# An output piece that no longer ends its stage: a hybrid trunk layer on one core, with two tiles and one flag moved

## The chip, the cores and the metric

The kernel runs on one NeuronCore of a Trainium2 chip. The time is that of one execution on the device, in microseconds; the figure of a kernel is the median of its runs. A profile is one more execution with the hardware profiler on; its span is the time from the first to the last instruction.

## What is computed

One layer of a streaming encoder over 2048 rows of 1024 channels, in float32. Cut to what matters here:

```
h = rmsnorm(x) * (1 + scale) + shift
p = h @ w_in                                  # one projection, cut among the branches
A = latent attention (8 heads, block-causal)  # softmax over all earlier rows
B = gMLP gating inside 128-row blocks
C = RWKV-7 recurrence over the rows           # chunked: 64-row chunks, state carried on
proj = each branch * silu(z) @ w_br           # three projections
merged = sum(proj * sigmoid(gate))
y = merged @ w_out
out = x + gate * rmsnorm(y)
```

## The kernel before

The 2048 rows are cut into four super-blocks of 512 (`s` = 0 to 3). For each `s` there are two stages, one after the other: `wkv(s)`, the recurrence of the super-block, and `attention(s)`. In the text they are recurrence 0 to 3 and attention 0 to 3. Each stage opens a pool of SBUF tiles (`pl`) and closes it at its end, so the tiles of the next stage can take the same memory.

All matrix products of 512 columns are made as three fp32r products of split operands (`mm3`: high by high, high by low, low by high). In the trace they are rows such as `pd<-hh,wh`, and the text calls them dense matmuls. The split weights are kept in DRAM (`kept`) and loaded again, 256 KB for the high and 256 KB for the low part of four k-tiles, that is for 12 dense matmuls (`again`, `wgran`). The ring that they are loaded into has nine places for high and low parts together; by the turns of its three tags the high part of a weight pair waits for the pair five before it to be used up, and the low part for the pair four before it.

TensorE's order is not written by hand. While the program is built, a planner (`Pace`) keeps generators ("threads") of ranks -1 to 4, estimates when each one's operands are ready, and lets one after the other issue its next step (`run`). The recurrence and the attention have low ranks; the projections that fill the gaps stand in two queues, `todo` (rank 3, what the next super-block needs first) and `later` (rank 4). The order that comes out is fixed: on the chip each engine works through its own list in that order and waits where an operand is late. SyncE issues nearly all DMAs, in its order too; a DMA that waits for a semaphore holds up every DMA behind it.

The last steps of a super-block, its three output pieces (`finish_units`), run as filler in the next recurrence: those of super-block `s - 1` in `wkv(s)`, for `s` = 1, 2 and 3. The last of them is `rows()`: it makes eight pieces of 128 x 512, for each of which it loads `y` and `x`, makes `y * rs + x` on VectorE, and stores to `out`. Its tiles come from the ring `f` of the stage's pool, three buffers for all its users. When all eight have been issued it sets `old[s, 3]`, and `wkv` ends only then:

```
pace.run(lambda: done[0] == 4 and (s == 0 or (s - 1, 3) in old), ...)   # line 1317, in wkv(s)
```

`done[0] == 4` says that the recurrence's four head pairs are issued. The recurrence's last steps on TensorE are the transpositions `pss<-consts,Y`; VectorE makes their result ready and SyncE stores it (`yr_d<-y`). Then `attention(s)` starts with the loads of its first head (`stg<-q_d`, `stg<-k_d`, `stg<-kp_d`, `vf<-v_d`), which ScalarE and GpSimd split into high and low parts (`qh`, `kh`; `ql`, `kl`), and its first matmuls are `pss<-kh,qh` and `pss<-kl,qh`. `x` and `y` of `rows()`, the weights and these loads all stand in SyncE's one list. Nearly every instruction is shown with line 120, that of the helper that records it.

Of the kernel before, what the change touches and what calls it, by code (L numbers as in the profile page):

```python
# [11 lines left out]
F32 = mybir.dt.float32  # L12
# [9 lines left out]
P = 128  # L22
# [284 lines left out]
def trunk(ctx, tc, io, out):  # L307
# [5 lines left out]
    def pool(name, bufs=1, space=None, stack=ctx):  # L313
        kw = {} if space is None else {"space": space}
        return pace.pool(stack.enter_context(tc.tile_pool(name=name, bufs=bufs, reuse_waits="tile", **kw)), bufs)
# [6 lines left out]
    sm = pool("sm", 2)  # L322
# [17 lines left out]
    def pt():  # L340
        return pace.ring("t", ps_t.tile([P, 512], F32, tag="t", name="pst"))
# [18 lines left out]
    def rstd_of(dst, src, mul, eps, n):  # L360

        tmp = sm.tile([P, 16], F32, tag="rst", name="rst", bufs=4)
        G.tensor_scalar(tmp[:, :n], src, mul, eps, op0=ALU.mult, op1=ALU.add)
        G.tensor_tensor(out=dst, in0=tmp[:, :n], in1=nhalf.broadcast_to([P, n]), op=ALU.pow)
# [215 lines left out]
    def gemm(w, c0, rhs, nk=KD, r0=0):  # L580

        yield (RD, *rhs[0])
        pace.lock = pace.cur
        o = pd()
        for kg in range(nk // 4):
            pace.early = EAR
            src = w[r0 + kg * 512:r0 + (kg + 1) * 512, c0:c0 + P].rearrange("(k p) c -> p k c", p=P)
            h, l = wgran((w.tensor.name, w.offset, r0 + kg * 512, c0), lambda raw: SY.dma_start(raw, src))
            pace.early = 0.0
            pace.forget(h, l)  # L590
            for k in range(4):
                kk = kg * 4 + k
                rh, rl = rhs[kk]
                yield (rh, rl)
                mm3(o, h[:, k, :], l[:, k, :], rh, rl, kk == 0, kk == nk - 1)
        pace.lock = None
        return o
# [96 lines left out]
    old = {}  # L694
# [866 lines left out]
    def operand(src, b):  # L1561

        yield ()
        for g in range(4):
            y = sm.tile([P, 512], F32, tag="z2", name="yg", bufs=3)
            SY.dma_start(y, src[g])
            b.append(br_split(y))
# [10 lines left out]
    def finish_units(s, pl):  # L1578

        bm, b0, b1 = [], [], []  # L1580
        ss = pl.tile([P, 4, 8], F32, name="ss")
        cnt = [0]

        def ft(name):
            return pl.tile([P, 512], F32, tag="f", name=name, bufs=FB)

        def merge(d):
            t = sm.tile([P, 512], F32, tag="gt", name="gt", bufs=2)
            SY.dma_start(t, gd[s % 2][0][d])
            q = ft("p12")  # L1590
            SY.dma_start(q, pp[s % 2][1][d])
            op = yield from gemm(w_br[0], d * P, bm, nk=4)
            V.scalar_tensor_tensor(t, t, 1.0, op, op0=ALU.add, op1=ALU.mult)
            ME.tensor_tensor(out=t, in0=t, in1=q, op=ALU.add)
            SY.dma_start(mg_d[s][d], t)

        def out0(e):
            o = yield from gemm(w_out, e * P, b0, nk=4)
            f = ft("yo")
            A.activation(f, o, AF.Copy)  # L1600
            SY.dma_start(yo_d[s][e], f)

        def out1(e):
            f = ft("yo")
            SY.dma_start(f, yo_d[s][e])
            gp = pl.tile([P, 1, P], F32, tag="gp", name="gp", bufs=2)
            SY.dma_start(gp[:, 0, :], gpg_d[:, e * P:(e + 1) * P])
            o = yield from gemm(w_out, e * P, b1, nk=4, r0=512)
            V.tensor_tensor(out=f, in0=o, in1=f, op=ALU.add)
            pace.spawn(1, back(e, f, gp))  # L1610

        def back(e, f, gp):
            yield (RT, f)
            o = pt()
            for j in range(4):
                PE.transpose(out=o[:, j * P:(j + 1) * P], in_=f[:, j * P:(j + 1) * P], identity=ident)
            jk = pl.tile([P, P], BF16, tag="jf", name="jf")
            for j in range(4):
                A.activation(jk, o[:, j * P:(j + 1) * P], AF.Square, accum_out=ss[:, j, e:e + 1])
            w = ft("yw")  # L1620
            V.tensor_tensor(out=w.rearrange("p (j c) -> p j c", j=4), in0=o.rearrange("p (j c) -> p j c", j=4),
                            in1=gp.broadcast_to([P, 4, P]), op=ALU.mult)
            SY.dma_start(y_d[s][:, e * P:(e + 1) * P].rearrange("(j p) c -> p j c", p=P), w.rearrange("p (j c) -> p j c", j=4))
            cnt[0] += 1
            if cnt[0] == 8:
                pace.spawn(0, rows())

        def rows():
            rs = sm.tile([P, 4], F32, tag="ors", name="ors")
            V.tensor_reduce(out=rs, in_=ss, axis=AX.X, op=ALU.add)  # L1630
            rstd_of(rs, rs, 1.0 / D, EPS, 4)
            for j in range(4):
                for i in range(2):
                    rows_, cs = slice(j * P, (j + 1) * P), slice(i * 512, (i + 1) * 512)
                    y, x = ft("y"), ft("x")
                    SY.dma_start(y, y_d[s][rows_, cs])
                    SY.dma_start(x, io["x"][0, s * SB + j * P:s * SB + (j + 1) * P, cs])
                    V.scalar_tensor_tensor(y, y, rs[:, j:j + 1], x, op0=ALU.mult, op1=ALU.add)
                    SY.dma_start(out[0, s * SB + j * P:s * SB + (j + 1) * P, cs], y)
                    yield (y,)  # L1640
            old[s, 3] = True

        return [[lambda: operand(ym_d[s], bm)] + [lambda d=d: merge(d) for d in range(8)],
                [lambda: operand(mg_d[s][0:4], b0)] + [lambda e=e: out0(e) for e in range(8)],
                [lambda: operand(mg_d[s][4:8], b1)] + [lambda e=e: out1(e) for e in range(8)]]
# [111 lines left out]
```

## Time and profile before

| | |
|---|---|
| median of 3 runs | 3095.43 us (3093.91 to 3096.95) |
| profiled execution, its own time | 3098.93 us |
| its span | 3096.6 us |
| granted TensorE clock, mean | 0.97 |
| TensorE busy (matmuls) | 2877.7 us, 93% of the span |
| VectorE busy | 1714.8 us, 55% |
| DMA queue of SyncE, share of 16 engines | 66.0% |

The profiled execution is 3.5 us longer than the median and 2.3 us longer than its span. "Busy" is time with an instruction in work; the idle time of an engine is listed before the instruction that ended it, with what that instruction waited for. The granted clock is a share of 2.4 GHz; a stretch at 1.2 GHz counts as half.

### The profile page before, as it was taken

The page shows a single profiled execution, that of the slowest core. Times are in us where ns is not written, and L with a number is a line of the kernel's source. Part 1 is how long each engine was busy: PE and PEld are TensorE (multiplying, and loading weights), DVE is VectorE, ACT ScalarE, POOL GpSimd, SP SyncE. Part 2 cuts the span into 40 slices and gives each one's busy share as a digit, 9 for nine tenths or more (in the row PEclk, how much of TensorE's full clock was granted, in tenths as well). Part 3 has the DMA queues.
Part 4 walks back from the last instruction along what each step waited for, and adds up shares of the span by engine and source line. Part 5 has one row for each costly group of instructions (what it writes and reads, how often), then busy time and mean ns, then how long its engine had stood idle before and what let it go on. Part 6 is the DMA issues. An engine that isn't in the chain of part 4 may idle for free.

```text
span 3096.6 us, 49478 instructions
## 1 busy us (share of the span) xinstructions
PE 2877.7 (93%) x16924; PEld 2330.6 (75%) x16924; DVE 1714.8 (55%) x4574; ACT 1235.2 (40%) x2868; POOL 598.8 (19%) x606
## 2 busy tenths in 40 slices
PE   5889988989989999999999998998899999899998
PEld 4667766777867777878877777887787677788886
DVE  6426675466257753466357653446645765356653
ACT  4325433444233433444333323454433333267641
POOL 3122232332021211131011101113100110222210
PEclk8999999989999999999999999999999999999999
DMA  7888755877766689765665578655557556844456
GB/s 270 260 273 252 223 176 164 268 237 244 231 211 196 198 252 286 223 203 173 211 210 174 167 236 266 201 164 187 160 168 243 179 158 215 263 143 134 124 183 218
DMA packets 521383, 645.84 MB, mean 209 GB/s; under 512 B 142160, under 2 KB 254892, under 8 KB 521132
## 3 DMA queue, kind: packets, MB, share of 16 engines
q1 hardware_dynamic: 520960, 642.64, 66.0%
q8 instruction: 134, 2.20, 0.3%
q14 instruction: 117, 0.96, 0.1%
q10 hardware_dynamic: 172, 0.05, 0.0%
HBM read 457.69 MB, written 184.81 MB: 207 GB/s over the span
## 4 chain that ended last, share of the span: by engine, by line
PE 59%; DVE 5%; DMA 4%; ACT 2%; issue 1%; POOL 1%; SPq 1%; POOLq 0%; DVEq 0%; ACTq 0%
PE pd L120 36%; PE pss L120 10%; PE pst L120 9%; PE pso L120 4%; DMA x<-in_x 1%; SPq L120 1%; DVE X L120 1%; DVE tx L120 0%; DMA tg<-gate_d 0%; DMA wr<-in_w_out 0%; DMA wl<-kept 0%; DMA yo<-yo_d 0%; ACT Y L120 0%; DMA xtb<-xd 0%; DMA wh<-kept 0%
## 5 line engine op out<-in xcount | busy, mean ns | idle before, releaser
L120 PE MATMUL pd<-hh,wh 128*128 128x512 f32 x1952 | 810.6, 415 | 16.7 <-ACT wh L120 6.4
L120 PE MATMUL pd<-hh,wl 128*128 128x512 f32 x1952 | 775.2, 397 | 7.8 <-POOL wl L120 5.9
L120 PE MATMUL pd<-hl,wh 128*128 128x512 f32 x1952 | 773.9, 396 | 2.8 <-DVE hl L120 1.8
L120 PEld LDWEIGHTS pd<-hh,wh 128*128 128x128 f32 x1952 | 373.3, 191 | 105.5 <-issue 13.2
L120 PEld LDWEIGHTS pd<-hh,wl 128*128 128x128 f32 x1952 | 372.2, 191 | 95.6 <-POOL wl L120 9.7
L120 PEld LDWEIGHTS pd<-hl,wh 128*128 128x128 f32 x1952 | 374.5, 192 | 71.1 <-DVE hl L120 3.6
L120 DVE TENSOR_TENSOR pw<-pst,ph 128x512 fp32r<-128x512 f32 (+2 forms) x352 | 196.3, 568 | 248.9 <-ACT ph L120 247.5
L120 ACT ACTIVATE ph<-pst 128x512 fp32r<-128x512 f32 (+2 forms) x352 | 171.5, 497 | 247.6 <-PE pst L120 211.2
L120 PE MATMUL pd<-brh,wh 128*128 128x512 f32 x576 | 252.3, 438 | 18.8 <-DVE gt L120 9.0
L120 PE MATMUL pd<-brh,wl 128*128 128x512 f32 x576 | 229.8, 399 | 0.6 <-POOL wl L120 0.6
L120 PE MATMUL pd<-brl,wh 128*128 128x512 f32 x576 | 230.2, 400 | 0.0
L120 DVE TENSOR_SCALAR_CACHE_REDUCE p<-pss 128x512 f32<-128x512 f32 (+2 forms) x320 | 191.2, 607 | 69.2 <-PE pss L120 65.2
L120 ACT ACTIVATE p<-p,nm 128x512 f32<-128x512 f32 (+3 forms) x288 | 189.7, 660 | 82.8 <-DVE nm L120 82.4
L120 POOL TENSOR_TENSOR wl<-wr,wh 128x512 fp32r<-128x512 f32 x98 | 131.2, 1341 | 435.4 <-ACT wh L120 347.5
L120 ACT ACTIVATE wh<-wr 128x512 fp32r<-128x512 f32 x162 | 101.1, 628 | 230.3 <-PE pd L120 89.0
L120 PE MATMUL pst<-consts,p 128*128 128x128 f32 x1088 | 162.4, 274 | 10.7 <-DVE za L120 5.8
L120 PE MATMUL pso<-ph,v 128*128 128x256 f32 x576 | 152.8, 288 | 0.0
L120 PEld LDWEIGHTS pd<-brh,wh 128*128 128x128 f32 x576 | 111.2, 193 | 52.3 <-issue 13.8
L120 PEld LDWEIGHTS pst<-consts,p 128*128 128x128 f32 x1088 | 128.8, 141 | 27.3 <-issue 12.0
L120 PE MATMUL pso<-pw,v 128*128 128x256 f32 x576 | 146.4, 283 | 1.2 <-DVE pw L120 1.2
L120 PE MATMUL pss<-kh,qh 96*128 96x512 f32 (+2 forms) x320 | 129.3, 404 | 18.2 <-ACT kh L120 15.2
L120 POOL TENSOR_TENSOR kl<-stg,kh 96x512 fp32r<-96x512 f32 x80 | 103.4, 1296 | 220.5 <-ACT kh L120 214.2
(295 smaller groups left out, 4820.7 us busy)
## 6 DMA issues: line engine op xcount, KB each, us to landing
wh<-kept SPq DMA_DIRECT2D x486, 256.0 KB
wl<-kept SPq DMA_DIRECT2D x486, 256.0 KB
kept<-wh SPq DMA_DIRECT2D x162, 256.0 KB
kept<-wl SPq DMA_DIRECT2D x162, 256.0 KB
wr<-in_w_in SPq DMA_DIRECT2D x120, 256.0 KB
gate_d<-gt SPq DMA_DIRECT2D x64, 256.0 KB
part_d<-gt SPq DMA_DIRECT2D x64, 256.0 KB
p<-part_d SPq DMA_DIRECT2D x64, 256.0 KB
```

Source lines behind the costliest of these rows:

```text
L120: r = f(*a, **k)
```

## The change

`old[s, 3]` is set when `rows()` starts instead of when it ends, and the tiles `y` and `x` of `rows()` come from the pool `sm`, which stays open through all stages, with one buffer each, instead of from the stage's ring `f`. So `wkv(s)` may end when the recurrence is done and `rows()` has begun, and the rest of the eight pieces is issued in `attention(s)`. The computation is the same.

```diff
             rs = sm.tile([P, 4], F32, tag="ors", name="ors")
             V.tensor_reduce(out=rs, in_=ss, axis=AX.X, op=ALU.add)
             rstd_of(rs, rs, 1.0 / D, EPS, 4)
+            old[s, 3] = True
             for j in range(4):
                 for i in range(2):
                     rows_, cs = slice(j * P, (j + 1) * P), slice(i * 512, (i + 1) * 512)
-                    y, x = ft("y"), ft("x")
+                    y, x = (sm.tile([P, 512], F32, tag=n, name=n[1], bufs=1) for n in ("ry", "rx"))
                     SY.dma_start(y, y_d[s][rows_, cs])
                     SY.dma_start(x, io["x"][0, s * SB + j * P:s * SB + (j + 1) * P, cs])
                     V.scalar_tensor_tensor(y, y, rs[:, j:j + 1], x, op0=ALU.mult, op1=ALU.add)
                     SY.dma_start(out[0, s * SB + j * P:s * SB + (j + 1) * P, cs], y)
                     yield (y,)
-            old[s, 3] = True
```

What the planner makes of it: TensorE's list is the same, instruction for instruction, but for three stretches, each from the end of a recurrence (1, 2 and 3) to the end of the attention behind it. Between the last transposition of the recurrence and the first matmul of the attention there stood 243, 198 and 198 dense matmuls; now there stand 45, 36 and 30. The others stand inside the attention and behind it: runs of 96, 81 and 123 dense matmuls now end the three stretches. The number of separate runs of dense matmuls in the three stretches goes from 151, 131 and 99 to 174, 139 and 113. (24 matmuls of two weight pairs go from the second stretch to the first.)

TensorE at the passage from recurrence 2 to attention 2, before: the last dense matmuls and the first three of the attention (`wh` and `wl` are the weight pair, `kh`, `kl`, `qh`, `ql` the split key and query).

```order
L120 MATMUL pd_19646<-hh_13728,wl_19668 128x512 [waits DMAHW5_49]
L120 MATMUL pd_19646<-hh_13730,wh_19667 128x512
L120 MATMUL pd_19646<-hl_13731,wh_19667 128x512
L120 MATMUL pd_19646<-hh_13730,wl_19668 128x512
L120 MATMUL pss_19677<-kh_19569,qh_19562 128x512 [waits PE_49,Activation_49]
L120 MATMUL pss_19677<-kl_19570,qh_19562 128x512 [waits Pool_49]
L120 MATMUL pss_19677<-kh_19569,ql_19563 128x512
```

And now, at the same place:

```order
L120 MATMUL pd_19406<-hh_14191,wl_19408 128x512
L120 MATMUL pd_19406<-hh_14193,wh_19407 128x512
L120 MATMUL pd_19406<-hl_14194,wh_19407 128x512
L120 MATMUL pd_19406<-hh_14193,wl_19408 128x512
L120 MATMUL pss_19427<-kh_19313,qh_19306 128x512 [waits PE_49,Activation_49]
L120 MATMUL pss_19427<-kl_19314,qh_19306 128x512 [waits Pool_49]
L120 MATMUL pss_19427<-kh_19313,ql_19307 128x512
```

The three matmuls wait for the same things as before, but the pair ahead of them is `wh_19407`, the third pair behind the recurrence's last transposition, where it was the seventeenth.

SyncE's list at the same passage, before, from the store of the last of the eight pieces to the attention's first load:

```order
L120 DMA out<-y_19495 128x512 [waits DMAHW0_49,DVE_49]
L120 DMA wh_19804<-kept_3861 128x512 [waits DMAHW1_49,PE_49]
L120 DMA yg_21833<-yr_d2_365 128x512 [waits DMAHW2_49]
L120 DMA wl_19805<-kept_3862 128x512 [waits DMAHW3_49,PE_49]
L120 DMA stg_19560<-q_d2_325 96x512 [waits DMAHW4_49]
```

And now, from the load of the third piece's `y` to the attention's first load:

```order
L120 DMA y_19270<-y_d1_360 128x512 [waits DMAHW6_49,DMAHW3_49]
L120 DMA wl_19424<-kept_2724 128x512 [waits DMAHW4_49,PE_49]
L120 DMA x_19271<-in_x 128x512 [waits DMAHW5_49]
L120 DMA wh_19463<-kept_2892 128x512 [waits PE_49]
L120 DMA wl_19464<-kept_2893 128x512 [waits DMAHW7_49,PE_49]
L120 DMA yr_d2_365<-y_19295 128x512 [waits DMAHW0_49,DVE_49]
L120 DMA out<-y_19270 128x512 [waits DMAHW1_49,DVE_49]
L120 DMA ut_19288<-sg_d2_341 128x512 [waits DMAHW2_49,DVE_49]
L120 DMA x_19391<-in_x 128x512 [waits DMAHW5_49,DMAHW3_49]
L120 DMA stg_19304<-q_d2_325 96x512 [waits DMAHW4_49]
```

The attention's first load stood behind the store of the eighth piece; now it stands behind the store of the recurrence's last tile and of the third piece. Five of the eight pieces are behind it. In stage 1 it is behind the fourth piece's store, in stage 3 behind the load of the fourth piece's `y`.

## Rows read from the trace of the kernel before

**Rows 1.** The profile's page, its first part: busy time of each engine, its share of the span, and its number of instructions.

```profile
PE 2877.7 (93%) x16924; PEld 2330.6 (75%) x16924; DVE 1714.8 (55%) x4574; ACT 1235.2 (40%) x2868; POOL 598.8 (19%) x606
```

**Rows 2.** Busy time of each engine in four stretches (microseconds from the span's start; behind each engine's busy time its number of instructions), with the granted TensorE clock as a share of full speed, the mean busy share of the 16 DMA engines and what they moved. First the last 46 us of the recurrence stage of super-block 2, then the first 18 us of attention 2 and of attention 3, then the passage from recurrence 0 to attention 0.

```profile
core 0: us, PE busy (x) PEld busy (x) DVE busy (x) ACT busy (x) POOL busy (x), PEclk, DMA share, GB/s
1848.00:1894.00 46.00, 45.37 (x202) 37.48 (x202) 17.13 (x26) 7.13 (x12) 0.00 (x0) 1.00 0.90 302
1894.00:1912.00 18.00, 9.76 (x29) 7.16 (x29) 1.81 (x7) 6.41 (x13) 7.09 (x7) 0.72 0.70 206
2682.00:2700.00 18.00, 9.66 (x29) 7.03 (x28) 1.97 (x5) 4.75 (x10) 8.92 (x9) 0.72 0.63 159
578.00:600.00 22.00, 19.71 (x79) 16.04 (x78) 6.57 (x23) 11.66 (x28) 7.44 (x9) 0.84 1.02 322
```

**Rows 3.** TensorE in order of time at the passage from recurrence 2 to attention 2: start, duration, engine, line, operation, out<-in, partitions x elements; in brackets the idle time before the instruction and what ended it. The first row is the last transposition of the recurrence, the next two are the ends of a run of 57 dense matmuls, the last two are the first matmuls of the attention.

```profile
1848.63 0.63 PE L120 MATMUL pss<-consts,Y 128*128 128x128 f32 x4 [0.85 <-DVE Y L120]
...
1855.03 0.39 PE L120 MATMUL pd<-hh,wl 128*128 128x512 f32 x1
...
1867.73 0.39 PE L120 MATMUL pd<-hl,wh 128*128 128x512 f32 x1
...
1901.20 0.80 PE L120 MATMUL pss<-kh,qh 96*128 96x512 f32 x1 [7.02 <-ACT kh L120]
1903.21 0.80 PE L120 MATMUL pss<-kl,qh 96*128 96x512 f32 x1 [1.22 <-POOL kl L120]
```

**Rows 4.** The same view at the passage from recurrence 3 to attention 3. The last row is the last of 14 single 512-column matmuls (the first is that of 2690.25) whose duration is above 0.55 us.

```profile
2637.26 0.60 PE L120 MATMUL pss<-consts,Y 128*128 128x128 f32 x4
...
2690.25 0.79 PE L120 MATMUL pss<-kh,qh 96*128 96x512 f32 x1 [7.45 <-ACT kh L120]
2691.93 0.79 PE L120 MATMUL pss<-kl,qh 96*128 96x512 f32 x1 [0.89 <-POOL kl L120]
...
2692.94 0.63 PE L120 MATMUL pd<-hh,wh 128*128 128x512 f32 x1
2693.37 0.63 PE L120 MATMUL pd<-hl,wh 128*128 128x512 f32 x1
...
2697.21 0.56 PE L120 MATMUL pd<-brl,wh 128*128 128x512 f32 x1
```

**Rows 5.** The same view at the passage from recurrence 1 to attention 1.

```profile
1153.72 0.63 PE L120 MATMUL pss<-consts,Y 128*128 128x128 f32 x4 [0.51 <-DVE Y L120]
...
1209.28 0.40 PE L120 MATMUL pss<-kh,qh 96*128 96x512 f32 x1
...
1218.64 0.50 PE L120 MATMUL pss<-kh,qh 96*128 96x512 f32 x1 [3.00 <-DVE p L120]
```

**Rows 6.** SyncE's DMA queue in order of time (start, duration of the issue) at the passage from recurrence 2 to attention 2.

```profile
1855.21 0.34 SPq L120 DMA_DIRECT2D out<-y  x1
...
1856.07 0.48 SPq L120 DMA_DIRECT2D yr_d<-y  x1
...
1886.21 0.41 SPq L120 DMA_DIRECT2D x<-in_x  x1
...
1891.67 0.34 SPq L120 DMA_DIRECT2D out<-y  x1
...
1893.51 0.42 SPq L120 DMA_DIRECT2D stg<-q_d  x1
```

**Rows 7.** The same queue at the two other passages: the store of the recurrence's last tile in stage 1 and in stage 3.

```profile
1158.01 0.32 SPq L120 DMA_DIRECT2D yr_d<-y  x1
...
2643.77 0.46 SPq L120 DMA_DIRECT2D yr_d<-y  x1
```

**Rows 8.** ScalarE in order of time: the first split of the query tile in attention 2.

```profile
1899.96 0.63 ACT L120 ACTIVATE qh<-stg 96x512 fp32r<-96x512 f32 x1 [11.88 <-DMA stg<-q_d]
```

**Rows 9.** The passage from recurrence 0 to attention 0, TensorE and SyncE's DMA queue: the last transposition of the recurrence, the store of its last tile, the first load of the attention, and the first two matmuls of the attention.

```profile
578.48 0.60 PE L120 MATMUL pss<-consts,Y 128*128 128x128 f32 x4
...
581.41 0.32 SPq L120 DMA_DIRECT2D yr_d<-y  x1
...
584.39 0.33 SPq L120 DMA_DIRECT2D stg<-q_d  x1
...
590.06 0.33 PE L120 MATMUL pss<-kh,qh 96*128 96x128 f32 x1 [0.75 <-ACT kh L120]
591.92 0.48 PE L120 MATMUL pss<-kl,qh 96*128 96x128 f32 x1 [1.54 <-POOL kl L120]
```

**Rows 10.** What ended VectorE's and the other engines' idle time before the 46 instructions that touch the tile `ors` (the row scales of an output piece): total microseconds, times; the row of the loads of `x`.

```profile
  DMA x<-in_x: 38.7, 16
```

**Rows 11.** What SyncE's DMA queue waited for from 1840 to 1894 us: total, times, longest.

```profile
SPq L120 <- DVE y L120: 13.1, 6, 3.1
SPq L120 <- PE pd L120: 12.2, 12, 1.6
SPq L120 <- DMA out<-y: 0.8, 1, 0.8
```

**Rows 12.** What TensorE waited for inside attention 2, from 1915 to 2301 us (the longest row).

```profile
PE pd L120 <- DVE gt L120: 6.9, 4, 3.9
```

**Rows 13.** TensorE inside attention 3: four transpositions and the two dense matmuls behind them.

```profile
2719.46 0.48 PE L120 MATMUL pd<-hh,wh 128*128 128x512 f32 x1
2719.78 0.40 PE L120 MATMUL pd<-hl,wh 128*128 128x512 f32 x1
```

## The prediction

> **What bounds the kernel now.** I read the page's busy times first: TensorE is busy for 2877.7 us, 93% of the span [rows 1], and no other engine comes near. So time can only come out of TensorE's idle time, or out of the stretches in which it runs at its lower clock. Next I looked at the end of a recurrence stage, because that is where the change cuts. The last 46 us of recurrence 2 look like waiting for the eight pieces, since the stage may not end before the eighth. But TensorE is busy for 45.37 of these 46 us at full clock [rows 2]: the planner has put filler there, and in it a dense matmul starts every (1867.73 - 1855.03) / 56 = 0.227 us [rows 3]. That filler has to be done at some time. Taking it out of the tail and putting it elsewhere saves nothing by itself.
>
> What is lost stands just behind the tail. The first matmul of attention 2 waits 7.02 us for the split key and the second another 1.22 us [rows 3]; in attention 3 it is 7.45 and 0.89 us [rows 4]. There is a second price. Behind the gap the dense matmuls start 0.43 us apart (2692.94 to 2693.37) instead of 0.227, that is at the lower of the two clock levels, 1.2 instead of 2.4 GHz, for 14 matmuls up to 2697.21 [rows 4]; 14 x 0.2 = 2.8 us. The granted clock of the two stretches is the same, 0.72 [rows 2], so I take 2.8 us for both. Attention 1 starts without a gap, and its first one, 3.00 us, comes 9 us later [rows 5]; with a smaller share for the clock, an estimate of 1.0 us, it costs 4.0. Together the three passages cost 4.0 + (7.02 + 1.22 + 2.8 = 11.0) + (7.45 + 0.89 + 2.8 = 11.1) = 26.1 us. That is all the change can win at the places that it aims at.
>
> **The change part by part.** *The moved filler.* TensorE's instructions are the same in number and kind, so the moved dense matmuls cost what they cost before: nothing. But they now stand in more runs: 426 instead of 381 in the three stretches. Behind four transpositions the second dense matmul starts 0.32 us after the first, not 0.227 [rows 13]. So a new run costs between 0 and 0.09 us; 45 runs, 0 to 4 us. I take the middle, +2 us.
>
> *When the attention's first key is ready.* Call T the start of the recurrence's last transposition. The first matmul of the attention now stands 45, 36 and 30 dense matmuls behind it; with 0.35 us for the transpositions TensorE gets there at T + 10.6, T + 8.5 and T + 7.2 us. When is the key there? From the issue of the query's load to the first matmul it took 1901.20 - 1893.51 = 7.7 us [rows 3, 6], of which 6.4 are the load itself [rows 6, 8]; at recurrence 0 it was 590.06 - 584.39 = 5.7 [rows 9]. I take 7.7, since the DMA engines are as busy there as in the tails [rows 2]. So the question is when SyncE issues that load, and here its list decides, because every DMA waits behind those ahead of it.
>
> In stage 2 the load stands behind the store of the third piece, and that needs the piece's `x`, whose load stands behind `wl_19424`. By the ring's turns that low part waits for the weight pair four before it, `wh_19257`, which is used up at T. So `x` is issued at T + 0.4 at the earliest. From the issue of an `x` to the store of its piece it took 1891.67 - 1886.21 = 5.5 us [rows 6]; the store is issued at T + 5.9, and after two more loads the query at T + 7. Key at T + 14.7, TensorE there at T + 8.5: a gap of 6.2 us, then again 1.2 us for `kl` and 2.8 us for the clock: 10.2 instead of 11.0.
>
> In stage 3 it stands behind the `y` of the fourth piece, and that must wait until the third piece has been stored, because `y` has one buffer. The low part of `wh_27834` just ahead of it is free only when the third weight pair behind T is used up, T + 5.1. I take T + 6.5: key at T + 14.2, gap 7.0, with 0.9 and 2.8 us 10.7 instead of 11.1.
>
> In stage 1 it stands behind the recurrence's last store, which came at 1158.01 - 1153.72 = T + 4.3 [rows 5, 7], and behind the fourth piece. I take T + 5.5: key at T + 13.2, gap 2.6, 1.3 for `kl`, 2.0 for the clock: 5.9 where 4.0 stood. The three passages together: +1.9 - 0.8 - 0.4 = +0.7 us.
>
> The bounds of this term. Below: recurrence 0 already passes to its attention in the new manner, without pieces. There the load is issued at T + 5.9, after the recurrence's store at T + 2.9, and the waits are 0.75 and 1.54 us [rows 9]; the clock of the 22 us is 0.84 [rows 2], which is 22 x 0.16 / 0.5 = 7 us at the lower level, some 5 of them in work, 2.5 us lost. 4.8 us each, 14.4 for three: -11.7. Above: the recurrence's store came at T + 7.4 in stage 2 and T + 6.5 in stage 3 [rows 3, 4, 6, 7]; with the load 1 to 2 us behind that, each gap grows by 2 us: +6.
>
> *The eight pieces.* Fourteen of the 24 are now issued inside the attentions. On VectorE each is 0.75 us in an engine that is busy 55% [rows 1]: nothing, with one exception. The first piece now stands between two state copies of the recurrence's last steps, because its `x` is there early. The chain of these copies can be held for up to 0.75 us per stage, 0 to 2.2 us; I take +0.5. On SyncE the `y` of a piece waits for the landing of the store before it. With two of three ring buffers in turn the queue waited 0.8 us for such a landing in the tail of stage 2, and 13.1 us in six waits for VectorE's pieces [rows 11], without a gap on TensorE; the weights are loaded four pairs ahead, that is over 10 us. I take nothing, and give the other case to a rival.
>
> The Trainium skill ("Trainium Kernel Development and Optimization", Best Practices) advises to double-buffer so that DMA and compute overlap, and this change goes the other way: one buffer for `y`, one for `x`. The trace agrees that the pieces live from their loads: VectorE's waits for `x` are 38.7 us in 16 [rows 10]. By that rule the pieces get slower, and the kernel would be slower where a piece still holds up something, the second rival.
>
> **The sum.** +2 + 0.7 + 0.5 = +3 us on a span of 3096.6: 3099.8, and with the 2.3 us around it 3102 against the profiled execution's 3098.93. That execution was 3.5 us above the median, so the median goes from 3095.4 to 3098.6. A measurement of this kernel can tell about 0.2%, 6.2 us, from no change.
>
> **The rivals.** *The gaps close* (faster). If the query's load comes as early as at recurrence 0, the passages cost 14.4 instead of 26.1 us: 3095.4 - 11.7 + 2 = 3086. For it: the new order is that of recurrence 0, and the third piece could be done early. Against it: `x` of that piece is behind a weight load that waits for T. Inside attention 2 the planner's new order could also avoid the 6.9 us of waits for `gt` [rows 12], with the same result. 0.23.
>
> *The pieces hold up the attention* (slower). SyncE waits at the head of its list for a store to land and for VectorE, up to 3.1 us at a time [rows 11], and behind it stand the keys of the next head. Fourteen pieces do this where TensorE has less filler ahead than in the tail. A wait that reaches TensorE costs like that of attention 1, 4.0 us; two such waits pass the 6.2 us, four give 3095.4 + 16 = 3111. For it: in stage 3 even the first query's load stands behind such a landing. Against it: the weights' lead. 0.31.
>
> *Nothing to tell*, my forecast: the filler is neutral, and the gaps stay because the loads stay late. 0.46; its own range is 3090 to 3101.
>
> **How the numbers follow.** Predicted 3099. The range for 8 in 10 reaches down past the closed gaps to 3081 and up past four or five held waits to 3114. Faster 0.23, same 0.46, slower 0.31.
>
> **What would show it.** In the trace after: the tails' long dense runs shortened to 8 to 11 us; gaps before the first `pss<-kh,qh` of 2 to 8 us in attentions 1, 2 and 3, ended by `kh`, each followed by matmuls at the lower clock; the query's load 5 to 7 us behind the last transposition; some 80 to 120 dense matmuls in a row, without idle time, at the end of each stretch. I am wrong if these gaps are under 1 us (then the first rival), or if TensorE shows new waits of 2 us and more for keys or weights inside the attentions (then the second).

## The result and the profile after

The changed kernel takes 3112.32 us (median of 6 runs, 3106.24 to 3121.99); the kernel before 3095.25 us (6 runs, 3089.79 to 3101.14). The ratio is 1.0057 with a 95% interval of 1.0042 to 1.0072: the change costs 17 us. The time lies in the predicted range (3081 to 3114), but the likeliest case, no change that can be told, did not come true.

The profiled execution took 3109.96 us, 11.0 more than that of before, with a span of 3107.7 us. TensorE's busy time, first part of the page, against [rows 1]:

```profile
PE 2886.2 (93%) x16924; PEld 2335.1 (75%) x16924; DVE 1715.4 (55%) x4573; ACT 1245.7 (40%) x2876; POOL 601.0 (19%) x607
```

The number of matmuls is the same, and TensorE is busy 8.5 us longer; slowed matmuls and the time lost in short runs count as busy. Where the time went can be read from TensorE's rows in order of time, cut at the starts T1, T2 and T3 of the last transpositions of recurrences 1, 2 and 3, and at the end of its last matmul:

| us | start to T1 | T1 to T2 | T2 to T3 | T3 to the last matmul |
|---|---|---|---|---|
| before | 1153.7 | 694.9 | 788.6 | 448.8 |
| after | 1150.5 | 699.6 | 785.0 | 462.1 |
| dense matmuls moved | 0 | +24 | -24 | 0 |

Up to T1 TensorE has the same list in both, so the 3.2 us there are scatter between executions. T1 to T3 together differ by 1.1 us. All that is clear is behind T3: 13.3 us.

First the three passages: TensorE, the last transposition of the recurrence and the first matmuls of the attention (as in [rows 3 to 5]).

```profile
1150.51 0.63 PE L120 MATMUL pss<-consts,Y 128*128 128x128 f32 x4 [0.49 <-DVE Y L120]
...
1161.86 0.49 PE L120 MATMUL pss<-kh,qh 96*128 96x512 f32 x1 [0.48 <-ACT kh L120]
...
1850.10 0.63 PE L120 MATMUL pss<-consts,Y 128*128 128x128 f32 x4 [0.45 <-DVE Y L120]
...
1863.95 0.80 PE L120 MATMUL pss<-kh,qh 96*128 96x512 f32 x1 [5.02 <-ACT kh L120]
1865.62 0.80 PE L120 MATMUL pss<-kl,qh 96*128 96x512 f32 x1 [0.87 <-POOL kl L120]
...
2635.12 0.60 PE L120 MATMUL pss<-consts,Y 128*128 128x128 f32 x4
...
2649.83 0.79 PE L120 MATMUL pss<-kh,qh 96*128 96x512 f32 x1 [7.26 <-ACT kh L120]
```

The same passages in SyncE's DMA queue: the load of the query.

```profile
1156.04 0.42 SPq L120 DMA_DIRECT2D stg<-q_d  x1
...
1856.35 0.44 SPq L120 DMA_DIRECT2D stg<-q_d  x1
...
2642.10 0.46 SPq L120 DMA_DIRECT2D stg<-q_d  x1
```

The load stands at T + 5.5, T + 6.3 and T + 7.0 us. In stage 1, where the attention began without a gap before, it is now 0.5 us; that of stage 2 is 5.0 us where it was 7.0, that of stage 3 is 7.3 where it was 7.5.

Then the end of stage 3. The attention's last transposition comes at 2978.49 us, 28.4 us earlier than before (3006.87), but 123 dense matmuls now stand behind it. 96 of them belong to the eight branch parts (`part`, n = 2) of super-block 3. What TensorE waited for from 2978 us on (total, times, longest; the longest row):

```profile
PE pd L120 <- DVE gt L120: 13.4, 3, 6.5
```

and for the kernel before, from 3007 us on (the two longest rows):

```profile
PE pd L120 <- DVE tg L120: 3.2, 2, 3.0
PE pd L120 <- ACT mh L120: 2.1, 2, 1.2
```

One of these waits, on TensorE and VectorE (start, duration, idle time before in brackets):

```profile
3003.25 0.80 PE L120 MATMUL pd<-brh,wh 128*128 128x512 f32 x1 [5.37 <-DVE gt L120]
3003.85 0.63 PE L120 MATMUL pd<-brl,wh 128*128 128x512 f32 x1
3004.27 0.63 PE L120 MATMUL pd<-brh,wl 128*128 128x512 f32 x1
...
3002.51 0.69 DVE L120 SCALAR_TENSOR_TENSOR gt<-gt,pd 128x512 f32<-128x512 f32 x1 [8.33 <-DMA gt<-gate_d]
```

The busy times of the stretches around it:

```profile
core 0: us, PE busy (x) PEld busy (x) DVE busy (x) ACT busy (x) POOL busy (x), PEclk, DMA share, GB/s
2960.00:2978.00 18.00, 18.00 (x117) 16.17 (x116) 6.33 (x13) 6.30 (x13) 0.00 (x0) 1.00 0.41 132
2978.00:3003.00 25.00, 18.42 (x82) 14.58 (x80) 3.25 (x5) 1.72 (x3) 2.58 (x2) 0.99 0.85 277
3003.00:3024.00 21.00, 14.23 (x49) 11.15 (x49) 2.95 (x5) 0.00 (x0) 5.26 (x5) 0.74 0.81 262
```

The product (`pd`) has to be read by VectorE before its buffer comes free; VectorE needs the gate tile `gt`, and the gate tile is late from DRAM. Behind the waits of 5.4 and 6.5 us come 14 and 13 matmuls that start 0.42 us apart, that is at the lower clock. A part is only 12 dense matmuls (2.7 us), but it loads a gate, an earlier part and a weight pair and stores its result, five transfers of 256 KB. Inside the attention the DMA engines are busy 0.41, in this run 0.81 to 0.85. The time from the attention's last transposition to the last matmul went from 79.2 us (3006.87 to 3086.0) to 118.7 us (2978.49 to 3097.2): 39.6 us for 123 matmuls, 0.322 each instead of 0.227.

So I went on with this theory: the loss is the run of parts behind attention 3, and the rest is about even. The rival was that of the prediction, pieces that hold up each attention through SyncE's list.

### The profile page after: what moved, and what is told of

It reads as the page before. It is cut to its first block, busy times and chain, and to the rows that moved or that the text cites. A ratio compares the mean times of both kernels' runs of the same rounds, so it can differ in the third digit from the quotient of the medians.

```text
span 3107.7 us, 49468 instructions
## 1 busy us (share of the span) xinstructions
PE 2886.2 (93%) x16924; PEld 2335.1 (75%) x16924; DVE 1715.4 (55%) x4573; ACT 1245.7 (40%) x2876; POOL 601.0 (19%) x607
## 4 chain that ended last, share of the span: by engine, by line
PE 57%; DVE 6%; DMA 4%; ACT 2%; issue 2%; POOL 1%; SPq 1%; POOLq 0%; DVEq 0%; ACTq 0%
PE pd L120 35%; PE pss L120 9%; PE pst L120 8%; PE pso L120 4%; SPq L120 1%; DVE X L120 1%; DVE tx L120 1%; DMA x<-in_x 1%; DMA gt<-gate_d 1%; DMA stg<-q_d 0%; ACT p L120 0%; DMA yo<-yo_d 0%; DMA vf<-v_d 0%; ACT Y L120 0%; POOL rs L120 0%
```

## The experiments

**Where it is lost.** The flag early in two of the three stages, or only in the third (there the condition is `s == 2`); the tiles are those of the change in both.

```diff
-            old[s, 3] = True
+            if s < 2:
+                old[s, 3] = True
             for j in range(4):
...
                     yield (y,)
+            old[s, 3] = True
```

> The flag is set early for the pieces of super-blocks 0 and 1 only; recurrence 3 ends, as before, with the eighth piece. Everything else is as in the changed kernel. Theory (the whole loss is the run of branch parts behind attention 3): stages 1 and 2 came out even within a few us, so 3092 to 3098 us, ratio 0.999 to 1.001. Rival (in each of the three attentions the pieces hold up keys through SyncE's list): two thirds of the loss of 17 us stay, about 3106 us, ratio 1.0037.

Measured: 3096.88 us (12 runs; before 3094.23), ratio 1.0003, interval 0.9989 to 1.0018.

> The flag is set early for the pieces of super-block 2 only, that is in recurrence 3; stages 1 and 2 end as before. Theory: the whole loss is here, 3106 to 3112 us, ratio 1.0035 to 1.0055, and TensorE again shows 10 to 14 us of waits for the gate tile behind attention 3. Rival (pieces hold up every attention): a third of the loss, about 3101 us, ratio 1.002.

Measured: 3104.61 us (12 runs), ratio 1.0028, interval 1.0015 to 1.0041; TensorE's waits for the gate tile behind attention 3 are 12.0 us. The time lies between the two forecasts. The larger share is in stage 3, and the theory's place is right. But 1.0028 and 1.0003 together fall short of the 1.0057 of the whole, by as much as the intervals just allow. Either that is chance, or a part that both kernels share, the tiles, wins time; the last experiments test the tiles alone.

**Spread the parts over the attention.**

```diff
-SHARE = [3.0, 2.0, 1.2, 0.5]
+SHARE = [3.0, 2.0, 1.2, 0.8]
```

> The changed kernel, with the planner's share of filler in attention 3 raised from 0.5 to 0.8: all eight branch parts then stand inside attention 3 (663 dense matmuls in it instead of 540) and the run behind it has 198 instead of 321. Theory: the parts find their loads done in the attention, the waits for the gate tile go from 13.4 to under 4 us, and some 10 to 15 us come back: 3096 to 3102 us, ratio 1.000 to 1.002. Rival (the loss comes from pieces in the attention or from more runs of dense matmuls): no gain, 3108 to 3115 us.

Measured: 3120.26 us (6 runs; before 3094.23), ratio 1.0075, interval 1.0053 to 1.0096. The waits for the gate tile are gone, as expected, and nothing came back: the attention itself now takes 41.3 us longer (369.9 from its first matmul to its last transposition, against 328.7), where its 123 further dense matmuls alone would take 27.9 at 0.227 each. The step "the time comes back when the parts stand inside" was wrong, and so I asked what filler costs inside an attention.

**The same share in the kernel before.** There the number of dense matmuls in attention 3 and around it stays the same, only their order changes.

> The kernel before, with only the planner's share in attention 3 raised from 0.5 to 0.8: the same 495 dense matmuls in attention 3, the same 198 ahead of it and behind it, but in 147 runs instead of 98. If filler costs more the more often it is cut (from the third experiment's attention 3: 75 more runs, 6 us more in work and 6 us more in small waits): 49 runs cost 6 to 8 us, 3100 to 3104 us, ratio 1.0017 to 1.0028. If a moved dense matmul is neutral, as predicted: ratio 0.999 to 1.001.

Measured: 3111.32 us (6 runs; before 3093.63), ratio 1.0056, interval 1.0033 to 1.0078. Twice what was expected, and the larger part has another reason than the number of runs. Here are attention 3's last three heads (limits taken at every 60th of the 480 `pso` matmuls), with the instructions on the tile `pd` alone, that is on TensorE the dense matmuls (first busy time and count; then weight loads, VectorE, ScalarE, granted clock, DMA share, GB/s). First the kernel before:

```profile
2900.20:2937.60 37.40, 14.75 (x54) 9.72 (x54) 0.00 (x0) 1.18 (x2) 1.00 0.38 113
2937.60:2974.10 36.50, 14.10 (x51) 9.09 (x51) 0.84 (x2) 1.17 (x2) 1.00 0.40 120
2974.10:3005.00 30.90, 18.14 (x66) 11.53 (x67) 3.95 (x6) 0.00 (x0) 1.00 0.68 207
```

Then this one:

```profile
2922.90:2961.70 38.80, 15.00 (x51) 8.95 (x51) 3.43 (x5) 0.00 (x0) 1.00 0.62 196
2961.70:2991.40 29.70, 0.00 (x0) 0.00 (x0) 0.00 (x0) 0.00 (x0) 1.00 0.08 23
2991.40:3013.70 22.30, 0.00 (x0) 0.00 (x0) 0.00 (x0) 0.00 (x0) 1.00 0.01 1
```

And its last two heads with all instructions (columns as in [rows 2]):

```profile
2961.70:2991.40 29.70, 27.11 (x181) 23.31 (x180) 23.26 (x73) 21.78 (x58) 3.50 (x5) 1.00 0.08 23
2991.40:3013.70 22.30, 18.82 (x132) 15.74 (x130) 13.07 (x31) 13.41 (x33) 0.00 (x0) 1.00 0.01 1
```

In the kernel before the seventh and eighth heads hold 51 and 66 dense matmuls; less 0.227 us for each, their own work takes 36.5 - 11.6 = 24.9 and 30.9 - 15.0 = 15.9 us. With the larger share the filler is used up before them, and the same work takes 29.7 and 22.3 us, 11.2 us more; the whole attention takes 14.9 us more (332.5 against 317.6 from its first matmul to its last transposition). TensorE is idle in them for 6.1 us, waiting for VectorE and ScalarE. So filler in an attention is no neutral load: it fills waits of the attention as long as there is some at that place. In the changed kernel with that share (the third experiment) it runs out too, in the eighth head, which holds 27 dense matmuls instead of 69 and takes 28.0 us net of them instead of 15.9 in the changed kernel. That is 12 us, the size of the gain that did not come.

**What the run of parts waits for.** First more gate tiles, then fewer transfers.

```diff
+            if s == NSB - 1 and d % 2:
+                t = sm.tile([P, 512], F32, tag=("ry", "rx")[d // 2 % 2], name="gt", bufs=1)
+            else:
                 t = sm.tile([P, 512], F32, tag="gt", name="gt", bufs=2)
```

> The changed kernel, in which the eight branch parts of super-block 3 have four tiles for the gate instead of two (the two tiles of the pieces, free by then, are added in turn); TensorE's list is unchanged. If the run waits because of its two buffers: the waits for the gate tile go from 13.4 to under 4 us, 3098 to 3104 us. If it waits because of the bytes (five transfers of 256 KB for 2.7 us of matmuls, 1.31 MB; at the 312 GB/s of 3024 to 3050 us that is 4.2 us, eight times 1.5 us too long = 12 us): only the two tiles ahead are won, 0.5 MB or 1.7 us, the waits stay at 9 us or more, 3108 to 3112 us.

Measured: 3116.97 us (6 runs; before 3094.23), ratio 1.0065, interval 1.0045 to 1.0085. TensorE's waits behind attention 3:

```profile
PE pd L120 <- DVE gt L120: 6.9, 4, 3.9
PE pd L120 <- DVE tg L120: 6.4, 4, 2.4
```

Both forecasts missed: the wait for `gt` was halved and moved to `tg`, the gate tiles of the merges that follow. All idle time there was 14.3 us in the changed kernel and is 15.3 now. It is not the number of gate tiles.

```diff
-            SY.dma_start(t, gd[s % 2][1][d])
+            if s < NSB - 1:
+                SY.dma_start(t, gd[s % 2][1][d])
...
-            SY.dma_start(q, pp[s % 2][0][d])
+            if s < NSB - 1:
+                SY.dma_start(q, pp[s % 2][0][d])
...
-        V.scalar_tensor_tensor(t, t, 1.0, op, op0=ALU.add, op1=ALU.mult)
-        if n == 2:
+        if n == 2 and s == NSB - 1:
+            A.activation(t, op, AF.Copy)
+        else:
+            V.scalar_tensor_tensor(t, t, 1.0, op, op0=ALU.add, op1=ALU.mult)
+        if n == 2 and s < NSB - 1:
             G.tensor_tensor(out=t, in0=t, in1=q, op=ALU.add)
```

> The changed kernel; left out are, for super-block 3, the loads of the gate and of the earlier part in its eight branch parts, and the arithmetic with them (the part is a copy of the product). Each part then moves three transfers of 256 KB instead of five. If the run behind attention 3 is slow because of its bytes (0.79 MB at 312 GB/s = 2.5 us for 2.7 us of matmuls): TensorE's waits there go from 14 us to 3 us or less, no matmuls at the lower clock, 3098 to 3104 us. If it is slow because of something else in the run (the split of the branch, the stores, the weights alone): waits of 8 us and more stay, 3108 to 3114 us.

Measured: 3094.84 us (10 runs; before 3093.63), ratio 1.0000, interval 0.9984 to 1.0016. Behind attention 3 no wait for a gate is left; 46 us of that run, and 46 us of the same run in the changed kernel:

```profile
2987.00:3033.00 46.00, 46.00 (x207) 38.13 (x206) 12.28 (x19) 9.67 (x16) 0.00 (x0) 1.00 0.93 314
```

```profile
2978.00:3024.00 46.00, 32.64 (x131) 25.73 (x129) 6.20 (x9) 1.72 (x3) 7.84 (x7) 0.88 0.83 270
```

Without the two loads TensorE is never idle in it, and the time from the attention's last transposition to the last matmul is 98.8 us instead of 118.7. VectorE's idle time above was ended by the gate's load, so the loads of the parts are the cause of the waits; VectorE's product and GpSimd's sum, left out with them, are not tested by themselves. Whether the loads do it by their bytes alone stays open: in the changed kernel the DMA engines moved 270 GB/s at a share of 0.83, less than the 314 at 0.93 here, and SyncE's list itself waited in those 46 us, 5.6 us for GpSimd's sum and 4.0 us for stores of parts to land. So the order of loads and stores, each behind the other, may have a part in it.

**Set the flag later.** If a shorter tail must only cover the query's load, it can be set when the seventh piece is issued.

```diff
-            old[s, 3] = True
             for j in range(4):
...
+                    if 2 * j + i == 6:
+                        old[s, 3] = True
                     yield (y,)
```

> The changed kernel with the flag set when the seventh piece is issued, not the first. The tails then have 183, 141 and 141 dense matmuls (before 243, 198, 198; changed kernel 45, 36, 30), the run behind attention 3 has 198 as before, and the query's load stands three to four weight pairs behind the recurrence's last store instead of behind the eighth piece. Theory (the tail's filler must be long enough to cover the load, 141 x 0.227 = 32 us against some 14 + 7.7 us; and the parts must not stand behind attention 3): the gaps before attentions 2 and 3 (7.0 and 7.5 us, and the lower clock behind them) are gone, 3072 to 3085 us, ratio 0.993 to 0.997. Rival (what moves is paid back elsewhere in the attentions): 3092 to 3098 us.

Measured: 3100.46 us (12 runs; before 3093.63), ratio 1.0027, interval 1.0011 to 1.0042. The forecast failed. In stage 3 the query's load stands at T + 11.6, as meant, but the key's stands behind two more pieces, at T + 27.9, and of the gap 2.9 us are left (in stage 2 1.8):

```profile
2682.41 0.62 SPq L120 DMA_DIRECT2D stg<-k_d  x1
...
2690.09 0.53 PE L120 MATMUL pss<-kh,qh 96*128 96x512 f32 x1 [2.89 <-ACT kh L120]
```

The rest of the loss is not settled; attention 1 shows a wait of 5.3 us for `h` where before it was 0.5, and one of 3.8 us for `p` where it was 3.0 [rows 5].

**The tiles alone** (the eighth experiment). The flag goes back to the end, the tiles stay as in the change.

```diff
-            old[s, 3] = True
             for j in range(4):
...
                     yield (y,)
+            old[s, 3] = True
```

> Only the tiles of the pieces are changed (one buffer each outside the stages); the flag is set at the end, as before, and TensorE's list is that of before. Theory: the single buffers cost nothing, since the pieces end beside 198 dense matmuls: 3092 to 3098 us, ratio 0.999 to 1.001. Rival (the second rival's price is in the single buffers: the pieces get slower, and the tail waits for the last of them): 3100 us or more, ratio over 1.0015.

Measured: 3084.28 us (12 runs; before 3093.63), ratio 0.9971, interval 0.9955 to 0.9986. Neither theory had a gain here. The same kernel was run again:

> The eighth experiment's kernel once more. If its gain is real: ratio 0.9955 to 0.9985, and 20 to 30 us below the changed kernel beside it. If it was chance: ratio 0.999 to 1.001.

Measured, on another chip beside the next two: 3090.87 us (12 runs; before 3095.99), ratio 0.9982, interval 0.9970 to 0.9995. The gain is real, 5 to 9 us. Its trace (the profiled execution of the eighth experiment was the longest of its 12, so I read the repeat) at the passage to attention 2, and four rows of SyncE's queue in stage 3, from the recurrence's last store on:

```profile
1847.29 0.60 PE L120 MATMUL pss<-consts,Y 128*128 128x128 f32 x4
...
1893.20 0.50 PE L120 MATMUL pss<-kh,qh 96*128 96x512 f32 x1 [0.37 <-ACT kh L120]
...
2639.05 0.38 SPq L120 DMA_DIRECT2D yr_d<-y  x1
...
2644.69 0.38 SPq L120 DMA_DIRECT2D stg<-q_d  x1
...
2650.64 0.34 SPq L120 DMA_DIRECT2D out<-y  x1
...
2656.66 0.49 SPq L120 DMA_DIRECT2D stg<-k_d  x1
```

From the transposition to the attention's first matmul it takes 45.9 us; before it took 52.6 [rows 3]. The gap of 7 us has gone although the flag is where it was. The query's load has moved: before it stood behind the store of the eighth piece [rows 6], now it stands ahead of the last five stores, at T + 11.7. But the stages end only 2.9 and 2.0 us sooner than before (T2 to T3 785.7 us, T3 to the last matmul 446.8), although their first matmuls come 6.7 and 7.6 us sooner. Part of it is given back behind the first matmul, where TensorE now waits for later keys. From 1893 to 2296 us, in attention 2 (the first head's 0.4 and 0.8 us included):

```profile
PE pss L120 <- POOL kl L120: 2.6, 3, 0.9
PE pss L120 <- ACT kh L120: 2.4, 3, 1.3
```

In attention 3 these waits are 1.9 and 2.9 us; in the kernel before attentions 2 and 3 show none behind the first head's two.

The next kernel differs from this one in one word: the same ring lies in the stage's pool.

```diff
-                    y, x = (sm.tile([P, 512], F32, tag=n, name=n[1], bufs=1) for n in ("ry", "rx"))
+                    y, x = (pl.tile([P, 512], F32, tag=n, name=n[1], bufs=1) for n in ("ry", "rx"))
```

> As the eighth experiment (tiles of the pieces in a ring of their own, one buffer each, flag at the end), but the ring lies in the recurrence stage's pool, not in the pool that stays open. If the gaps ahead of attentions 2 and 3 closed there because the attention's first tiles no longer wait for memory that the pieces hold: the query's load stands behind the eighth piece's store again, the gaps of about 7 us come back, 3092 to 3098 us, ratio 0.999 to 1.001. If they closed because the pieces have a ring of their own and run at another pace: no gaps, 3081 to 3088 us, ratio 0.996 to 0.998.

Measured: 3108.09 us (12 runs; before 3095.99), ratio 1.0033, interval 1.0019 to 1.0047. With the ring in the stage's pool the load is back behind the eighth store, and the gap is larger than before:

```profile
2641.86 0.60 PE L120 MATMUL pss<-consts,Y 128*128 128x128 f32 x4
...
2698.93 0.80 PE L120 MATMUL pss<-kh,qh 96*128 96x512 f32 x1 [11.09 <-ACT kh L120]
...
2689.72 0.34 SPq L120 DMA_DIRECT2D out<-y  x1
...
2691.60 0.38 SPq L120 DMA_DIRECT2D stg<-q_d  x1
```

The two kernels differ only in the pool, so it is the pool that lets the load pass. The likely reason, which no run shows by itself: the attention's first tiles take the memory of the recurrence's pool, and a load into them waits for what still uses it. The pieces were among that; outside the stage they are not. This kernel also shows the price of the single buffers: the eighth piece is stored at T + 47.9 instead of T + 43.1 (2680.33, before), in stage 2 at T + 51.8 instead of 43.0, and the kernel is 12 us slower than before. By the Trainium skill ("Trainium Kernel Development and Optimization", Best Practices) one should double-buffer so that DMA and compute overlap; here the trace agrees, with 4.8 and 8.7 us a stage, where the next stage waits for the pieces, and with the tiles alone, where the next stage does not wait for them, the single buffers leave no gap of more than 0.4 us ahead of an attention.

Last, the tiles alone with the first head's loads further ahead, and the change once more.

```diff
-            for _ in prologue(0):
-                pass
+            with tc.high_priority(offset=100):
+                for _ in prologue(0):
+                    pass
```

> The eighth experiment's kernel, with the loads of each attention's first head placed earlier in SyncE's list (a higher priority for them). The query's load stays where it was; the position part of the key (kp_d) and v go ahead of one to three pieces. Theory (the last of these loads still lands just as TensorE arrives, and waits of some 1 to 2 us for kh and kl are left): 0 to 5 us faster than the eighth, 3079 to 3085 us, ratio 0.9955 to 0.9975. Rival (the pieces, now later, end after the filler): as slow as before or slower, ratio 0.999 and more.

Measured: 3086.22 us (12 runs; before 3095.99), ratio 0.9972, interval 0.9958 to 0.9986. As fast as the tiles alone within what can be told. The gaps for `kh` and `kl` are gone, and in stage 2's tail TensorE instead waits once for ScalarE, 3.9 us:

```profile
PE pd L120 <- ACT brh L120: 3.9, 1, 3.9
```

> The changed kernel once more, beside the next one on the same chip, to set the two halves of the change against each other: 3105 to 3118 us, ratio 1.004 to 1.007.

Measured: 3113.30 us (6 runs; before 3095.99), ratio 1.0050, interval 1.0032 to 1.0069. On one chip, then: before 3096, tiles alone 3091, tiles and flag 3113. The tiles win 5 us, and the early flag costs 22. With the first two experiments: beside the tiles alone (0.9971 and 0.9982) the flag in stage 3 costs 0.0046 to 0.0057 or 14 to 18 us, that in stages 1 and 2 0.0021 to 0.0032 or 6 to 10 us. Each of these has an interval of about 6 us to both sides. In the profiled executions of the two repeats the first share is clear (T3 to the last matmul 460.0 against 446.8 us), and the second is not: with the 24 moved matmuls allowed for at 5.4 us, -1.3 and +1.4 us in the stretches T1 to T2 and T2 to T3. All traces together show more. T1 to T3 takes 1477.6 to 1484.6 us in the six with the early flag in stages 1 and 2 (middle 1483.4), and 1476.6 to 1479.0 in the three with the tiles alone there (middle 1477.5; the flag early only in the third stage, and the tiles alone twice). Some 3.4 of these 5.9 us lie between T2 and T3. But one order of instructions scatters by as much: with the order of before in stages 1 and 2 two traces have 1477.5 and 1483.5.

## Why the prediction was right or wrong

**The passages: nearly right.** The query's load was put at T + 5.5, 7 and 6.5 us; it stood at 5.5, 6.3 and 7.0. The gaps were put at 2.6, 6.2 and 7.0 us; they are 0.5, 5.0 and 7.3, each but the first with the lower clock behind it. The forecast's "the gaps stay because the loads stay late" came true in stages 2 and 3. In stage 1 the first matmul came at T + 11.4 instead of T + 13.2: 5.8 us behind the load, not the 7.7 that I took from attention 2.

**The moved filler: the step that failed.** The term that was wrong in kind is "the moved dense matmuls cost what they cost before: nothing", with +2 us for the runs. In stage 3 168 dense matmuls left a tail in which each took 0.227 us without a wait. 45 went into the attention, 123 behind it, and the latter take 0.322 us, 11.7 us more in all. I counted TensorE's instructions and forgot what they bring along: the five transfers of a part were spread over attention 3, with DMA at 0.48 there, and now they come in one go. I had even written the sign down as "some 80 to 120 dense matmuls in a row, without idle time, at the end of each stretch". The number was right, the "without idle time" was not checked against the transfers. In stages 1 and 2 the runs at the end show no such waits. What the 45 further runs of dense matmuls cost by themselves, the +2 us, no run separates. That the time still lies in the range is luck: the range reaches so far up for pieces that hold up the attentions, not for this.

**The tiles: taken at nothing, in truth a gain.** The prediction gave the single buffers no price and the place of the tiles none. Their place moves the query's load past five pieces and closes the gaps of 7.0 and 7.5 us, with the flag as before; that is worth 5 to 9 us. The prediction had priced these two passages at 11.0 and 11.1 us, and that was too much for what closing them wins: some of it comes back as waits for later keys, and where the rest goes no run shows. The early flag then gives the gain away: it takes the tail that covers the load down to 36 and 30 dense matmuls, and the gaps are back.

**The second rival: its size by another mechanism, in the main.** 3111 us were named for pieces that hold up the attentions. The measured time is 3112, but 14 to 18 of the some 22 us that the flag costs arise in stage 3, and there the trace shows the run of parts, 13.4 us of waits, and a gap of 7.3 us that the tiles alone bring down to waits of 2.9 us. But its mechanism does show in attention 2, and with it the sign that the prediction named for it, a new wait of 2 us and more for a weight:

```profile
1892.22 0.47 PE L120 MATMUL pd<-hh,wh 128*128 128x512 f32 x1 [4.11 <-DMA wh<-kept]
...
1870.67 0.38 SPq L120 DMA_DIRECT2D stg<-q_d  x1
1876.96 0.34 SPq L120 DMA_DIRECT2D out<-y  x1
...
1888.11 0.45 SPq L120 DMA_DIRECT2D stg<-k_d  x1
...
1889.23 0.42 SPq L120 DMA_DIRECT2D wh<-kept  x1
```

SyncE's list waits 5.8 us for the fourth piece (until 1876.96), issues the weights and keys behind it, waits another 5 us until these keys have landed and been split and a key tile is free (1888.11), and only then loads the weight. The five other traces with the early flag in stage 2 show the same wait, 3.4 to 3.9 us. How much of it the piece costs, no run shows. In attention 2 the waits for `gt`, 6.9 us before [rows 12], are down to 2.2, as the first rival thought possible, and the waits for weights take their place, 4.7 us in two. The 6 to 10 us that the flag costs by the times in stages 1 and 2 thus lie most likely at this wait and the gap of 5.0 us ahead of attention 2, which the tiles alone bring to 0.4; that is argued from the traces, and no run tests it.

**The first rival** (gaps close, 3086 us) did not come by the flag. The tiles alone do close them, and their 3084 and 3091 us lie about there. It beats both kernels.

## What to carry to other kernels

Here tiles in a stage's pool held the next stage's first loads behind their last user; before moving the end of a stage, try the smaller step of moving the tile. When filler leaves a place where it was hidden, cost it with its transfers per matmul and with what it covers at both ends, not by TensorE's time alone. And where a change has two parts, time each by itself: here they had opposite signs.

## What the runs showed that was not expected

Filler that has run out is missed: the own work of the last two heads of attention 3 took 11.2 us longer without it (of that 6.1 us in idle time of TensorE), with every granted clock at 1.00. And the DMA engines moved 314 GB/s over 46 us beside TensorE without a wait, while the run of parts waited at 270 GB/s: here transfers came late while the engines moved less than they did elsewhere.
